# One dense tile of two RWKV quarters moved: from between the two lanes of the preparation to behind the first group of key-query products

## The chip, the cores and the metric

The kernel runs on one core of a Trainium2 chip. The metric is the device time in microseconds of one execution; of several runs the median is given. The engines are named as in the profile: PE is the matrix engine TensorE (PEld its weight loads), DVE is VectorE, ACT is ScalarE, POOL is GpSimd, and SP is the queue that issues most DMA transfers.

## The reference

One inference step of a one-layer hybrid decoder: 512 tokens of a prompt and 64 sampled tokens (8 sequences of 8), 576 in all, 1024 channels wide, in 32-bit floating point. The layer projects the normalised input once and splits the columns between two mixers. The Mamba-2 part convolves over time and runs a state space recurrence; the RWKV-7 part shifts the tokens and runs a matrix-valued recurrence per head (16 heads of 64 channels). The output projection, a SwiGLU block and a per-layer embedding follow. Cut to what the change touches:

```python
proj = hn @ w['w_in']
z, xbc, dt_raw, rw = jnp.split(proj, IN_SPLITS, axis=-1)
conv = lax.conv_general_dilated(concat([conv_buf, xbc]), conv_w, ...) + conv_b    # causal, 4 taps
xbc_act = silu(conv)                                  # 12 tiles of 128 channels
...
u = rw + (prev - rw) * shift_mu
r, k, v, w_lo, a_lo, g_lo = jnp.split(u, RWKV_SPLITS, axis=-1)
w_log = -softplus(-(w0 + tanh(w_lo) @ w2)) - 0.5      # decay, a low-rank product ("lora")
a = sigmoid(a0 + a_lo @ a2)                           # in-context rate, a second one
kk = normalised(k * k_k)
# S_t = S diag(w) - (S kk)(kk*a)^T + v k^T, read out with r; then a norm per head, a bonus, a gate
```

## The kernel before

**Tiles.** Activations lie transposed: a tile holds 128 channels by 576 tokens. A dense tile is 128 columns of the projection: 8 blocks of input channels, 2 halves of 288 tokens and 3 products each (values are split into a high and a low part, lines 228 to 230), 48 matmuls into one of the two buffers of the PSUM pool `lin`. Its weights come by DMA, are split on ACT and on DVE or POOL (line 213), and what follows depends on its kind: a tile of the convolution (`conved`) is copied out by ACT, gets three multiply-adds on DVE (line 402), a tanh and a product on ACT, two more products on DVE (lines 407 and 408) and four small copies on POOL (lines 393 to 396); a tile of the RWKV part (`shifted`) is mixed with the token before.

**Quarters and lanes.** The RWKV heads are worked in four quarters of 256 channels, `Q[0]` to `Q[3]`; the text counts them from nought as the code does, so quarters one and two are the second and the third. Each quarter has two lanes `jj` of 128 channels. Per quarter: `fill_for` runs dense tiles until the quarter's own six are there; `prep` makes decays, rates and normalised keys, lane by lane (two loras on PE, a scan at line 568, products at 572 to 588, line 591 on DVE and line 592 on POOL that write the keys `bk`); `gram` multiplies keys and queries on PE in five groups (line 620), each into a buffer of `lin`, from where DVE (line 630) and ACT with POOL (lines 641 and 645) take it out through masks; `bonus` (its products are at line 253); `solve` and `combine` invert small triangles (lines 674 to 719); `chain` runs the recurrence over chunks, each step from PE to DVE and back several times (lines 796 to 838).

**What sets the order.** The program is written in the order above, but a list scheduler puts the instructions on the engines' queues, from the written order, the pools' free buffers and a cost model. So the chain of a quarter lies beside the preparation of the next. A queue runs in its order: an instruction that waits holds what is behind it. The buffers of `lin` go round in the written order among dense tiles, loras, groups of products and the bonus.

**Where dense tiles are put.** `fill(n)` takes the next n tiles from a list that `projections` makes, whose order the change does not touch. `prep`, `gram` and `inverse` call it at eight places through `fill_at`, and the table `FP` gives for each quarter how many tiles each place takes: 0 after the sums of squares, 1 and 3 after the loras of the two lanes, 2 and 4 at the end of the two lanes, 5 and 6 after the first and the third group of products, 7 in the inverse. In quarters one and two the three tiles that the table places are all of the convolution. After the products of quarter one eight more dense tiles run, after those of quarter two six.

Of the kernel before, what the change touches and what calls it, by code (L numbers as in the profile page):

```python
# [49 lines left out]
GMA = (0, 0, 0, 0)  # L50
GMB = (0, 0, 0, 1)
FILL = (5, 5, 3, 0)
FP = ((1, 0, 1, 0, 1, 0, 0, 0), (1, 0, 1, 0, 1, 0, 0, 0), (1, 0, 1, 0, 1, 0, 0, 0), (0, 0, 0, 0, 0, 0, 0, 3))


def in_tiles(q):
# [19 lines left out]
def hybrid_step(ctx, tc, A):  # L76
# [401 lines left out]
    def fill(n=1):  # L478

        for _ in range(min(n, len(todo))):  # L480
            which, c = todo.pop(0)
            if which == "xbc":
                conved(c)
            elif which == "z":
                zed(c)
            elif which == "dt":
                dts()
            else:
                Q[which].t.append(shifted(c, which == 0, which % 2 and len(Q[which].t) > 3))

    def fill_at(s, i):
        fill(FP[s.q][i])

# [1253 lines left out]
```

## Time and profile before

| | |
|---|---|
| median of 3 runs | 1333.55 us (1332.72 to 1333.56) |
| profiled execution | 1329.48 us, span of its instructions 1327.7 us |
| mean granted clock of PE | 0.951 |
| busy in the span | PE 92%, DVE 67%, ACT 48%, POOL 46% |
| preparation and products of quarter one | about 208 to 268 us |
| preparation and products of quarter two | about 350 to 410 us |

Rows of groups give an instruction's line, engine, operation, output and inputs with their shapes, how often it ran, its busy time, the mean in ns of one, and the idle time of its engine ahead of it with what ended that. Rows of the chain of waits give the start, the time and the work that everything behind depended on. A matmul's duration reaches past the start of the next one, so the durations of a dense run add up to more than the time it takes. The clock is the share of TensorE's full clock that the chip granted.

### The profile page before, as it was taken

What the parts mean: (1) busy time and instruction counts of PE and PEld (TensorE: products, weight loads), DVE (VectorE), ACT (ScalarE), POOL (GpSimd) and SP (SyncE); (2) the same over time, 40 slices, a digit from 0 to 9 for tenths busy, and PEclk for the clock granted to TensorE, in tenths of its full rate; (3) what the DMA queues carried; (4) which work ended last, traced back from release to release, by engine and by line L of the source; (5) the groups of instructions that cost most, each with busy time, mean ns of one, the idle gap of its engine ahead of it and who ended that gap; (6) DMA issues with size and microseconds to landing.
All of it is one profiled execution on the core that took longest, in us unless ns stands there. A gap on an engine that the chain in (4) does not pass through costs nothing.

```text
span 1327.7 us, 26629 instructions
## 1 busy us (share of the span) xinstructions
PE 1224.9 (92%) x10429; PEld 1125.1 (85%) x10429; DVE 885.8 (67%) x1569; ACT 632.0 (48%) x1274; POOL 615.4 (46%) x584
## 2 busy tenths in 40 slices
PE   6897899999989978899989989999999999999997
PEld 5786797889968966788769878999999999999996
DVE  6649665878696876953456576858895138883464
ACT  6565436543654374343444364455553225553363
POOL 5426513642265136122445665647565345654642
PEclk9898999799978979979989989999999999999998
DMA  5322241334232322353454541253342224424322
GB/s 167 127 65 72 78 116 54 98 96 119 73 103 79 83 72 78 103 180 106 132 182 131 201 151 59 78 161 106 98 113 89 81 83 114 116 66 136 99 89 72
DMA packets 96764, 140.29 MB, mean 106 GB/s; under 512 B 34960, under 2 KB 39312, under 8 KB 96640
## 3 DMA queue, kind: packets, MB, share of 16 engines
q1 hardware_dynamic: 93760, 133.36, 32.6%
q0 software_dynamic: 2304, 4.72, 2.1%
q8 instruction: 82, 1.34, 0.4%
q10 hardware_dynamic: 576, 0.52, 0.1%
q14 instruction: 42, 0.34, 0.1%
HBM read 106.10 MB, written 27.75 MB: 101 GB/s over the span
## 4 chain that ended last, share of the span: by engine, by line
PE 58%; DVE 19%; ACT 6%; issue 6%; DMA 4%; POOL 3%; SPq 0%; DVEq 0%; ACTq 0%; POOLq 0%
PE lin L241 12%; PE lin L1432 11%; PE lin L228 6%; PE lin L230 6%; PE lin L229 6%; DVE h L402 2%; DVE wl L191 1%; DVE Tt L683 1%; DVE tmp L681 1%; DVE wlo L213 1%; PE lin L1577 1%; PE lin L1578 1%; PE lin L1579 1%; DVE suv L838 1%; DMA raw<-wts 1%
## 5 line engine op out<-in xcount | busy, mean ns | idle before, releaser
L213 POOL TENSOR_TENSOR wlo<-raw,whi 128x512 fp32r<-128x512 f32 (+1 forms) x92 | 125.8, 1368 | 303.6 <-ACT whi L93 235.0
L228 PE MATMUL lin<-xhi,whi 128*128 128x288 f32 (+1 forms) x784 | 242.1, 309 | 2.8 <-ACT whi L93 2.2
L230 PE MATMUL lin<-xhi,wlo 128*128 128x288 f32 (+1 forms) x784 | 240.2, 307 | 4.0 <-POOL wlo L213 2.3
L229 PE MATMUL lin<-xlo,whi 128*128 128x288 f32 (+1 forms) x784 | 239.6, 306 | 1.2 <-POOL xlo L191 1.1
L93 ACT ACTIVATE whi<-raw 128x512 fp32r<-128x512 f32 (+1 forms) x200 | 123.2, 616 | 211.0 <-PE lin L241 90.0
L228 PEld LDWEIGHTS lin<-xhi,whi 128*128 128x128 f32 (+1 forms) x784 | 149.5, 191 | 10.1 <-ACT whi L93 2.6
L230 PEld LDWEIGHTS lin<-xhi,wlo 128*128 128x128 f32 (+1 forms) x784 | 149.4, 191 | 7.9 <-POOL wlo L213 2.7
L229 PEld LDWEIGHTS lin<-xlo,whi 128*128 128x128 f32 (+1 forms) x784 | 149.4, 191 | 6.5 <-POOL xlo L191 2.4
L213 DVE TENSOR_TENSOR wlo<-raw,whi 128x512 fp32r<-128x512 f32 (+1 forms) x108 | 82.1, 761 | 74.2 <-PE lin L241 36.0
L1432 PE MATMUL lin<-T,wh 128*128 128x288 f32 x576 | 87.3, 296 | 2.0 <-DVE e L1477 1.3
L1432 PEld LDWEIGHTS lin<-T,wh 128*128 128x128 f32 x576 | 80.0, 189 | 3.2 <-DVE e L1477 1.6
L93 ACT ACTIVATE wh<-raw 128x512 fp32r<-128x512 f32 x72 | 45.1, 628 | 52.5 <-PE lin L1432 35.4
L191 POOL TENSOR_TENSOR wl<-raw,wh 128x512 fp32r<-128x512 f32 x36 | 57.3, 1592 | 11.7 <-ACT wh L93 6.2
L191 DVE TENSOR_TENSOR wl<-sw,wh 128x512 fp32r<-128x512 f32 x53 | 49.9, 941 | 9.3 <-ACT wh L93 5.2
L241 PE MATMUL lin<-ah,whi 128*128 128x288 f32 x352 | 54.7, 294 | 0.0
L241 PE MATMUL lin<-al,whi 128*128 128x288 f32 x352 | 54.4, 294 | 0.0
L241 PE MATMUL lin<-ah,wlo 128*128 128x288 f32 x352 | 54.2, 294 | 0.0
L681 DVE TENSOR_TENSOR tmp<-L,Tt 72x30 f32<-72x30 f32 (+14 forms) x120 | 49.9, 416 | 3.2
L1432 PE MATMUL lin<-T,wl 128*128 128x288 f32 x288 | 49.8, 297 | 0.6 <-DVE wl L191 0.6
L241 PEld LDWEIGHTS lin<-ah,whi 128*128 128x128 f32 x352 | 49.3, 188 | 0.0
L241 PEld LDWEIGHTS lin<-al,whi 128*128 128x128 f32 x352 | 49.2, 188 | 0.0
L241 PEld LDWEIGHTS lin<-ah,wlo 128*128 128x128 f32 x352 | 49.2, 188 | 0.0
(437 smaller groups left out, 3265.7 us busy)
## 6 DMA issues: line engine op xcount, KB each, us to landing
raw<-wts SPq DMA_DIRECT2D x271, 256.0 KB, 2.6
S<-s_wkv SPq DMA_DIRECT2D x8, 512.0 KB, 5.1
hd<-s_ssm SPq DMA_DIRECT2D x8, 512.0 KB, 4.6
o_ssm_s<-hd SPq DMA_DIRECT2D x8, 512.0 KB, 2.8
xbc_d<-E SPq DMA_DIRECT2D x12, 288.0 KB, 2.1
x<-xT SPq DMA_DIRECT2D x8, 288.0 KB
gate_d<-g SPq DMA_DIRECT2D x8, 288.0 KB, 2.5
bv_d<-rw SPq DMA_DIRECT2D x8, 288.0 KB
```

Source lines behind the costliest of these rows:

```text
L93: return S.activation(out, in_, func, bias=bias, scale=scale)
L191: eng.tensor_tensor(lo, src, hi.bitcast(F32), ALU.subtract)
L213: eng.tensor_tensor(lo[:, 0:n], raw[:, 0:n], hi[:, 0:n].bitcast(F32), ALU.subtract)
L228: T.matmul(ps[:, a:b], whi, xhi[:, a:b], start=first, stop=False)
L229: T.matmul(ps[:, a:b], whi, xlo[:, a:b], start=False, stop=False)
L230: T.matmul(ps[:, a:b], wlo, xhi[:, a:b], start=False, stop=last)
L241: T.matmul(ps[:, a:e], (hi, lo)[p][:, i * P:(i + 1) * P], xs[k + i][q][:, a:e], start=n == k + i == 0, stop=n == 2 and k + i == nk - 1, sk ...
L402: V.scalar_tensor_tensor(h[:], E[:, i:i + 600], w(i), h[:], ALU.mult, ALU.add)
L681: V.tensor_tensor(o, L[:, jx:jx + 1, jx + 1:32].to_broadcast([NB, jx, n]), Tt[:, 0:jx, jx:jx + 1].to_broadcast([NB, jx, n]), ALU.mult)
L683: V.tensor_tensor(Tt[:, 0:jx, jx + 1:32], Tt[:, 0:jx, jx + 1:32], o, ALU.subtract)
L838: V.scalar_tensor_tensor(dst, sv[h, jj, 0, e], PC[h, jj, 7 + g:8 + g], dw[h, jj], ALU.mult, ALU.add)
L1432: T.matmul(ps, (hi, lo)[p][:, k * P:(k + 1) * P], OPS[n][k][q], start=first and p == q == k == 0, stop=p == 1 and k == 3, skip_group_check ...
```

## The change

The rows of quarters one and two in the table change. The first dense tile stays after the sums of squares. The second leaves the place between the lanes (index 2) and comes at the end of the second lane (index 4); the third, which was there, comes after the first group of products (index 5). The tiles, their order among themselves and their number stay, and quarters nought and three keep their rows.

```diff
--- before.py
+++ after.py
@@ -50,7 +50,7 @@
 GMA = (0, 0, 0, 0)
 GMB = (0, 0, 0, 1)
 FILL = (5, 5, 3, 0)
-FP = ((1, 0, 1, 0, 1, 0, 0, 0), (1, 0, 1, 0, 1, 0, 0, 0), (1, 0, 1, 0, 1, 0, 0, 0), (0, 0, 0, 0, 0, 0, 0, 3))
+FP = ((1, 0, 1, 0, 1, 0, 0, 0), (1, 0, 0, 0, 1, 1, 0, 0), (1, 0, 0, 0, 1, 1, 0, 0), (0, 0, 0, 0, 0, 0, 0, 3))
 
 
 def in_tiles(q):
```

With the tile gone from between the lanes, the buffers of `lin` go round otherwise: before, the second lane's loras came after the second tile, now the four loras come one after another, then the second tile, the first group of products, the third tile and the second group.

PE, quarter one, between the lanes. `ulh` and `ull` are the operands of the loras, `xhi` and `xlo` those of a dense tile, `rx` is a transpose for the normalised keys, `um` and `suv` belong to the chain and the sampled tokens of quarter nought. Before:

```order
L530 MATMUL cb_2840<-ident,rx_2836 128x128 x4
L819 MATMUL cx_1732<-G_982,suv_1669 64x64 x4
L856 MATMUL cx_1744<-um_1745,bkt_1719 64x512
L228 MATMUL lin_2860<-xhi_350,whi_2863 128x288
L229 MATMUL lin_2860<-xlo_351,whi_2863 128x288
L856 MATMUL cx_1744<-um_1746,bkt_1719 64x512
L533 MATMUL cb_2846<-ident,rx_417_2838 128x128
L228 MATMUL lin_2942<-ulh_345,whi_2690 128x288
L229 MATMUL lin_2942<-ull_346,whi_2690 128x288
L230 MATMUL lin_2942<-ulh_345,wlo_2691 128x288
L228 MATMUL lin_2942<-ulh_345,whi_2690 128x288
L229 MATMUL lin_2942<-ull_346,whi_2690 128x288
```

With the change:

```order
L530 MATMUL cb_2840<-ident,rx_2836 128x128 x4
L228 MATMUL lin_2860<-ulh_345,whi_2690 128x288
L229 MATMUL lin_2860<-ull_346,whi_2690 128x288
L230 MATMUL lin_2860<-ulh_345,wlo_2691 128x288
L228 MATMUL lin_2860<-ulh_345,whi_2690 128x288
L229 MATMUL lin_2860<-ull_346,whi_2690 128x288
L230 MATMUL lin_2860<-ulh_345,wlo_2691 128x288
L819 MATMUL cx_1732<-G_982,suv_1669 64x64 x4
L856 MATMUL cx_1744<-um_1745,bkt_1719 64x512
L856 MATMUL cx_1744<-um_1746,bkt_1719 64x512
L533 MATMUL cb_2846<-ident,rx_417_2838 128x128
L228 MATMUL lin_2870<-ulh_345,whi_2690 128x288
```

The loras of the second lane come directly behind the transposes, and the dense tile that was begun there is gone.

PE, quarter one, around the second half of the products of group 0 (`lin_3117` before, `lin_3035` with the change). Before:

```order
L620 MATMUL lin_3117<-G_2686,bk_2986 128x128
L620 MATMUL lin_3132<-G_2686,bk_2986 128x128
L796 MATMUL cx_1859<-suv_1834,G_982 128x128
L620 MATMUL lin_3117<-G_2686,bk_2986 128x128
L620 MATMUL lin_3132<-G_2686,bk_2986 128x128
L620 MATMUL lin_3132<-G_2686,bk_2849 128x128 x2
L620 MATMUL lin_3132<-G_2686,bk_2986 128x128 x2
L804 MATMUL cx_1865<-xs_1862,TT_465 64x64 x4
L809 MATMUL cx_1870<-ar_981,suv_1834 64x64 x4
L620 MATMUL lin_3149<-G_2686,bk_2849 128x128 x2
L620 MATMUL lin_3149<-G_2686,bk_2986 128x128 x2
```

With the change:

```order
L620 MATMUL lin_3035<-G_2686,bk_2904 128x128
L804 MATMUL cx_1865<-xs_1862,TT_465 64x64
L228 MATMUL lin_3048<-xhi_461,whi_3081 128x288
L229 MATMUL lin_3048<-xlo_462,whi_3081 128x288
L230 MATMUL lin_3048<-xhi_461,wlo_3082 128x288
L228 MATMUL lin_3048<-xhi_461,whi_3081 128x288
L229 MATMUL lin_3048<-xlo_462,whi_3081 128x288
L804 MATMUL cx_1865<-xs_1862,TT_465 64x64 x3
L809 MATMUL cx_1870<-ar_981,suv_1834 64x64 x4
L620 MATMUL lin_3035<-G_2686,bk_2904 128x128
L230 MATMUL lin_3048<-xhi_461,wlo_3082 128x288
L819 MATMUL cx_1870<-G_982,suv_1834 64x64
```

The dense tile `lin_3048` runs ahead of and between the products of group 0 now; before, the products followed one another with only steps of the chain between them.

DVE, quarter two, from the second lane to the masks. `h` is the convolution's sum, `kk`, `pb`, `lo` and `bk` belong to the preparation, `suv` and `xs` to the chain, `Lst` takes the masked products. Before:

```order
L402 SCALAR_TENSOR_TENSOR h_4792<-E_4784,hw,h_4792 128x600
L586 SCALAR_TENSOR_TENSOR kk_4695<-lo_4682,kk_4695 128x576
L799 COPY xs_3520<-cx_3517 64x128
L402 SCALAR_TENSOR_TENSOR h_4792<-E_4784,hw,h_4792 128x600
L591 SCALAR_TENSOR_TENSOR bk_4709<-kk_4695,lo_4672 64x9x64 x2
L588 TENSOR_TENSOR lo_4682<-lo_4682,rw_4129 128x576
L407 SCALAR_TENSOR_TENSOR E_4784<-th_4797,h_4792 128x512
L408 SCALAR_TENSOR_TENSOR E_4784<-th_4797,h_4792 128x64
L812 TENSOR_SCALAR suv_3472<-cx_3523 64x2x64
L602 SCALAR_TENSOR_TENSOR lo_4682<-rw_4265,pv,lo_4682 128x576
L838 SCALAR_TENSOR_TENSOR suv_3538<-suv_3472,pc_2687,cx_3544 64x64 x4
L630 TENSOR_TENSOR Lst_4839<-lin_4840,dgmask 64x128 x2
```

With the change:

```order
L402 SCALAR_TENSOR_TENSOR h_4710<-E_4702,hw,h_4710 128x600
L588 TENSOR_TENSOR lo_4600<-lo_4600,rw_4129 128x576
L799 COPY xs_3566<-cx_3563 64x128
L407 SCALAR_TENSOR_TENSOR E_4702<-th_4715,h_4710 128x512
L408 SCALAR_TENSOR_TENSOR E_4702<-th_4715,h_4710 128x64
L602 SCALAR_TENSOR_TENSOR lo_4600<-rw_4265,pv,lo_4600 128x576
L213 TENSOR_TENSOR wlo_5594<-raw_5591,whi_5593 128x512
L630 TENSOR_TENSOR Lst_4757<-lin_4758,dgmask 64x128
L812 TENSOR_SCALAR suv_3538<-cx_3569 64x2x64
L402 SCALAR_TENSOR_TENSOR h_4843<-E_4835,hw,h_4843 128x600
L630 TENSOR_TENSOR Lst_4757<-lin_4758,dgmask 64x128
L402 SCALAR_TENSOR_TENSOR h_4843<-E_4835,hw,h_4843 128x600
```

Before, the last tile's convolution was over ahead of the first mask; now the tile before it stands at that place, and the last tile's stands between the masks.

## The prediction

> **What bounds the kernel now.** I read the page's totals first, then the windows of the stages that the change touches, then the chain of waits through them.
>
> ```profile
> span 1327.7 us, 26629 instructions
> ...
> PE 1224.9 (92%) x10429; PEld 1125.1 (85%) x10429; DVE 885.8 (67%) x1569; ACT 632.0 (48%) x1274; POOL 615.4 (46%) x584
> ...
> PEclk9898999799978979979989989999999999999998
> ...
> PE 58%; DVE 19%; ACT 6%; issue 6%; DMA 4%; POOL 3%; SPq 0%; DVEq 0%; ACTq 0%; POOLq 0%
> ```
>
> TensorE (PE) is the bound on average, but it holds only 58% of the chain that ends last, and its clock dips in single slices. So the average says nothing about the two places of the change, the preparations of quarters one and two. They are the first and the third row here; the second and the fourth are the stretches behind them, where dense tiles run, and the fifth is the chain of quarter two, where no dense tile is left. The last two are the groups of key-query products alone. The columns are the window, its length, each engine's busy time, the granted clock, the DMA share and GB/s.
>
> ```profile
> 208.00:268.00 60.00, 56.01 (x472) 45.94 (x471) 44.52 (x76) 38.48 (x82) 34.42 (x46) 0.83 0.24 76
> 268.00:341.00 73.00, 69.38 (x588) 64.55 (x586) 58.24 (x134) 28.13 (x68) 24.42 (x29) 1.00 0.39 113
> 350.00:410.00 60.00, 54.16 (x485) 44.31 (x483) 48.64 (x79) 38.08 (x81) 32.65 (x43) 0.83 0.23 75
> 410.00:470.00 60.00, 57.51 (x520) 52.82 (x520) 45.40 (x116) 21.52 (x56) 17.25 (x18) 0.97 0.38 104
> 470.00:527.00 57.00, 45.41 (x558) 34.02 (x554) 44.23 (x87) 34.83 (x80) 29.41 (x33) 0.88 0.19 57
> ...
> 256.00:268.00 12.00, 11.18 (x117) 9.55 (x115) 7.81 (x20) 7.19 (x21) 8.66 (x15) 0.64 0.08 27
> ...
> 399.00:410.00 11.00, 10.50 (x116) 8.95 (x112) 6.92 (x20) 7.74 (x22) 7.73 (x13) 0.75 0.06 21
> ```
>
> In both preparations the clock is 0.83, and it falls to 0.64 and 0.75 while the key-query products run: a busy TensorE there is a slow TensorE. Behind them the clock is 1.00 and 0.97 and TensorE is nearly full. The chain of waits says who holds the preparation of quarter two up (start, us, what):
>
> ```profile
> 372.63 1.54 DVE h L402
> ...
> 374.79 1.54 DVE h L402
> 376.33 2.50 DVE lo L568
> 378.83 1.86 DVE h L402
> ...
> 388.38 0.84 DVE h L402
> ...
> 391.10 0.75 DVE h L402
> ...
> 392.88 0.84 DVE h L402
> ...
> 395.19 0.76 DVE lo L588
> ...
> 396.46 1.42 DVE E L408
> ...
> 399.71 2.01 PE lin L620 x16
> ```
>
> VectorE (DVE) holds it. Six of these steps are L402, the convolution of a dense tile, which nobody in the preparation needs: it only stands on VectorE ahead of what is needed. L588 is the last VectorE work before GpSimd (POOL) makes the second half of the keys, and the products of group 0 that use it (L620) can only follow:
>
> ```profile
> 396.02 3.25 POOL L592 TENSOR_TENSOR bk<-lo,lo 64x576 f32<-64x576 f32 x2 [9.55 <-DVE lo L588]
> ```
>
> POOL had waited 9.55 us for L588 by then. Whatever convolution work leaves the queue ahead of L588 brings this point forward.
>
> **The change part by part.** Nothing is added or removed; each of the two quarters has its second dense tile moved to the end of the second lane and its third from there to behind group 0.
>
> *1. Convolutions ahead of L588.* Before, quarter two has three of them ahead of L588 but for the last L407 and L408; the order of the change has two there, with the third from the first masks (L630) on. So one tile's work leaves. Its price is in the groups of VectorE between 350 and 402 us, then between 208 and 260 us (busy, mean ns of one):
>
> ```profile
> L402 DVE SCALAR_TENSOR_TENSOR h<-E,hw,h 128x600 f32<-128x600 f32 x9 | 10.2, 1136 | 1.5 <-ACT h L93 1.4
> ...
> L407 DVE SCALAR_TENSOR_TENSOR E<-th,h 128x512 f32<-128x512 f32 x3 | 2.9, 965 | 0.0
> L213 DVE TENSOR_TENSOR wlo<-raw,whi 128x512 fp32r<-128x512 f32 x4 | 2.7, 686 | 0.7 <-ACT whi L93 0.7
> ...
> L408 DVE SCALAR_TENSOR_TENSOR E<-th,h 128x64 f32<-128x64 f32 x3 | 1.8, 616 | 0.0
> ```
>
> ```profile
> L402 DVE SCALAR_TENSOR_TENSOR h<-E,hw,h 128x600 f32<-128x600 f32 x9 | 9.4, 1040 | 1.7 <-ACT h L93 1.6
> ...
> L407 DVE SCALAR_TENSOR_TENSOR E<-th,h 128x512 f32<-128x512 f32 x3 | 3.0, 1014 | 0.0
> ...
> L408 DVE SCALAR_TENSOR_TENSOR E<-th,h 128x64 f32<-128x64 f32 x3 | 2.1, 697 | 0.0
> L213 DVE TENSOR_TENSOR wlo<-raw,whi 128x512 fp32r<-128x512 f32 x3 | 2.0, 682 | 0.0
> ```
>
> The new order takes from ahead of quarter two's L588 3 x 1.14 + 0.97 + 0.62 + 0.69 (the low part of a weight block) = 5.7 us. In quarter one the last tile's L402 stand behind L588 already; what leaves is one L402, L407, L408 and a weight split of the tile before: 1.04 + 1.01 + 0.70 + 0.68 = 3.4 us. Together -9.1 us. The other bound is 0: if something else becomes last in the lanes, all of it is lost.
>
> *2. The clock in the products.* A slow clock costs at most what is missing: 12.00 x (1 - 0.64) = 4.3 us in quarter one and 11.00 x (1 - 0.75) = 2.75 us in quarter two, 7.1 together. With a dense tile in front of the second half of group 0 TensorE is fuller there. Bounds 0 and -7.1.
>
> *3. The moved convolution beside the products.* In quarter one VectorE is busy 7.81 of 12.00 us. The tile adds about 4.9 (three L402, L407, L408 by the second set of rows), so 12.7 in 12.00; in quarter two 6.92 + 5.0 = 11.9 in 11.00. VectorE becomes the bound there and the stretch grows by 0.7 and 0.9, provided that the clock has recovered as in 2; otherwise by up to a tile's 5 us each. With the recovered clock the stage could not be shorter than that, so I take 2 and 3 together: +1.6 us. Bounds -7.1 and +10.
>
> A rule speaks against this step. Here L402 takes 1.54 to 1.86 us where POOL works beside it (the first rows of the chain) and 0.75 to 0.84 where it doesn't. The Trainium skill, "SBUF — State Buffer", section on its two sides, says that VectorE and GpSimd share one port pair under an exclusive lock, which an operation with two SBUF inputs takes against a GpSimd operation that reads SBUF, and that the loser waits for the whole instruction. By it the moved L402, beside POOL's masks, would cost 1.0 us more each, about +3 us a quarter; by the uncontended rows nothing more. The rows agree with the rule as to the doubling, but say nothing of masks as short as those; it is rival A.
>
> *4. Lanes without the tile between them.* The loras of the second lane come right behind those of the first, and wait for a buffer of the two in the lin pool, which ScalarE's tanh frees. The row of such a wait, the longest of TensorE between 208 and 269 us:
>
> ```profile
> PE lin L228 <- ACT lo L93: 1.6, 1, 1.6
> PE lin L230 <- POOL wlo L213: 1.1, 1, 1.1
> ```
>
> Behind a waiting lora stand the chain's small products of the quarter before. One more such wait of 1.6 us a quarter, of which VectorE's queue hides a part: +1 each, +2 together. Bounds 0 and, by the stretch that has no dense tiles at all, see rival B, +12.8.
>
> *5. What runs earlier.* In the new order 12 small products of the chain stand ahead of the bonus's first product (L253) in quarter one that stood behind it, and 18 in quarter two. Their groups between 268 and 341 us:
>
> ```profile
> L804 PE MATMUL cx<-xs,TT 64*64 64x64 f32 x24 | 2.3, 236 | 2.4 <-DVE xs L799 2.4
> L830 PE MATMUL cx<-suv,bkt 128*64 128x64 f32 x32 | 1.9, 234 | 0.0
> L819 PE MATMUL cx<-G,suv 128*64 128x64 f32 x32 | 2.9, 228 | 0.0
> ```
>
> At 0.23 us it is 2.8 and 4.1 us, but durations overlap: products start every 0.13 us in a dense run, so about half, 1.5 and 2.2. The stretch behind is shorter by that if TensorE ran them where it else idled. That it does is half sure: -1.9 us. Bounds 0 and -3.7.
>
> ```profile
> 205.03 0.29 PE L228 MATMUL lin<-xhi,whi 128*128 128x288 f32 x1
> 205.16 0.29 PE L229 MATMUL lin<-xlo,whi 128*128 128x288 f32 x1
> ```
>
> *Does it reach the end?* Behind the products TensorE is nearly full at clock 1.00 and 0.97, so an earlier start is an earlier end, unless the solve ends last. Its last VectorE copy is done long before its result is used (L705), 22 us in quarter two:
>
> ```profile
> L684 DVE COPY L<-Tt x1: 1091/1091/1091, 457.0 to 457.0; 36x1024 f32<-36x1024 f32 x1
> ...
> L705 PE MATMUL cx<-AA,Lst x64: 191/191/212, 479.1 to 480.1; 32*32 32x32 f32 x64
> ```
>
> In the new order its first operation (L674) stands one or two steps of the chain further back on VectorE, which this covers, as it does a shift of the whole size; the weight loads follow too, with a DMA share of 0.39 at most. The moved tile's own matmuls cost nothing extra, being moved from one TensorE-filled place to another; without that cover its 48 products are 48 x 0.13 = 6.3 us.
>
> **The sum:** -9.1 + 1.6 + 2 - 1.9 = -7.4 us. The profiled execution took 1329.48 us around its span of 1327.7, so it becomes 1322.1. The runs' median is 1333.55, 4.1 above the profiled one; the same difference gives 1326.1, and I say 1326.
>
> **Rivals.**
>
> *A, the stall only moves.* VectorE is taken out of the lanes and put between the masks, where a late L630 keeps a lin buffer and so the next group waiting. For it: 12.7 us of VectorE work in 12.00, and the doubled L402. Against: only the masks are delayed, and dense tiles are queued behind. With the extra 3 us a quarter the sum is -7.4 + 6 = -1.4; with an unrecovered clock about +1. So 1333 ± 2.7.
>
> *B, slower: the second lane loses its filler.* In the stretch from 470 us, without dense tiles, TensorE is busy 45.41 of 57.00 us at clock 0.88: 0.20 + 0.12 = 0.32 us lost in each. A lane of 12 to 20 us without a tile would lose 3.8 to 6.4 a quarter, 10.2 for both in the middle, in place of the +2 of step 4. If ScalarE's tanh or the transposes then hold the lane, half of step 1 is lost as well: -4.5 + 1.6 + 10.2 - 1.9 = +5.4, 1339. It decides once a quarter loses over 4.7 us more in the lane than step 4 has. For it: the clock is the lowest where only small products run. Against: the second tile follows at the end of the same lane, and the new order puts the loras, which are dense, there.
>
> The clock has a rule of its own: the Trainium skill, "TensorE: Matmul & The Clock Gate", section "HAM oscillation — how this bites in real kernels", asks for no TensorE idle gap over some 3.4 us. By it the waits of 1 to 2 us here would leave the clock alone, and B would lose 0.20 a us, not 0.32, so 1335; the trace differs, for the clock is 0.64 from 256 to 268 us with TensorE busy 11.18 of 12.00.
>
> *C, a larger gain.* The products run at full clock, VectorE's masks fit around the convolution and no wait is added: -9.1 - 7.1 - 3.7 = -19.9, 1314. For it: 7.1 us of missing clock. Against: VectorE's 12.7 us.
>
> *D, it does something else.* The order is made by a scheduler, and TensorE's rows differ from 218 to about 820 us. A queue that is put differently further on (the loras of quarter three) may add or take about 3 us. It widens the other cases.
>
> **How the numbers follow.** Forecast 0.54 (4 to 14 us gained, 1319.5 to 1329.5), A 0.16, B 0.20, C 0.10. A measurement of this kernel tells 0.2%, 2.7 us, from no change. Faster by more: forecast and C, 0.64; within: A, 0.16; slower: B, 0.20. The range takes in C's point and B's: 1314 to 1339, with half of each beyond, 0.15 left out; it lies inside the bounds of the steps.
>
> **What would show it.** Step 1: L588 of the second lane some 5 us nearer to the preparation's start in quarter two, some 3 us in quarter one. Steps 2 and 3: a clock near 1 from group 0 to L253, with L402 among the L630 and at about 0.8 us; at 1.5 us and more it is A. Step 4: one wait of a lora on ScalarE of under 2 us a quarter; several, with the clock under 0.8 in the second lane, are B. The end: the dense stretches as long as before, less a few us. If the time from the start of a preparation to L253 isn't shorter by 2 to 7 us in each quarter, I am wrong.

## The result, and the profile after

The change makes the kernel slower: 1346.28 us (median of 4 runs, 1342.0 to 1350.56) against 1333.13 us, a ratio of 1.0108 with a 95% interval of 1.0065 to 1.015. The profiled execution took 1344.57 us against 1329.48, with a span of 1342.8 against 1327.7. The forecast was 1326 us, in a range from 1314 to 1339.

The page of the changed kernel, the lines that answer to those shown of before:

```profile
span 1342.8 us, 26625 instructions
...
PE 1238.9 (92%) x10429; PEld 1136.9 (85%) x10429; DVE 884.5 (66%) x1569; ACT 629.9 (47%) x1272; POOL 612.3 (46%) x584
...
PEclk9897799999988976879989988999999999999998
...
PE 51%; DVE 14%; issue 4%; ACT 3%; DMA 3%; POOL 1%; SPq 0%; DVEq 0%; ACTq 0%; POOLq 0%
```

The work is the same (10429 matmuls, DVE 884.5 us against 885.8), so 15 us were added by waiting and by a slower clock. The page doesn't say where. Its last line, the chain of waits, can't be compared with that of before: its shares add up to 76%, those of before to 96%, so the chain was not followed back as far. I cut both spans at instructions that both kernels have: the first scan of a quarter (line 568), the end of line 588 in the second lane, the first product of the bonus (line 253), the first use of quarter three's solve (line 705), the end of the dense tile lin_9035, and the start of lin_9233, the first tile of the output projection's gated half that runs from its first product to its last without a stop. All in us:

| stretch | before | change | difference |
|---|---|---|---|
| start to quarter one's scan | 212.9 | 215.4 | +2.5 |
| quarter one, scan to L588 | 39.1 | 36.3 | -2.8 |
| quarter one, L588 to L253 | 16.2 | 20.1 | +3.9 |
| to quarter two's scan | 85.3 | 85.3 | 0 |
| quarter two, scan to L588 | 42.4 | 37.9 | -4.5 |
| quarter two, L588 to L253 | 14.3 | 18.3 | +4.0 |
| to quarter three's scan | 65.8 | 61.2 | -4.6 |
| quarter three, scan to L253 | 47.8 | 54.8 | +7.0 |
| to L705 | 59.2 | 60.8 | +1.6 |
| to the end of lin_9035 | 174.0 | 172.8 | -1.2 |
| to the start of lin_9233 | 47.8 | 58.7 | +10.9 |
| to the end of the span | 522.9 | 521.0 | -1.9 |

Up to quarter three's scan the change is 1.3 us ahead, although it lost 2.5 us ahead of quarter one's scan, where TensorE's order is still the same in both kernels; so much can differ between two profiles of the same order. It loses 7 us in quarter three, whose row in the table it does not touch, and 11 us some 300 us behind that, in the state space part.

The windows of these stretches, first of before and then of the change (window, length, busy times of PE, PEld, DVE, ACT and POOL, clock, DMA share, GB/s): the products of quarters one and two from L588 on, quarter three, its second half, and the stretch from the end of lin_9100 to lin_9233. lin_9100 is the last dense tile that needs nothing of the gated half; "the last dense tile" below means it.

```profile
252.10:268.20 16.10, 15.28 (x136) 12.67 (x133) 11.55 (x26) 8.80 (x25) 12.69 (x18) 0.61 0.12 37
395.90:410.20 14.30, 13.02 (x148) 11.21 (x146) 9.19 (x24) 7.91 (x23) 10.80 (x14) 0.70 0.06 23
...
476.00:523.80 47.80, 37.27 (x488) 27.91 (x488) 37.52 (x70) 27.44 (x63) 24.80 (x31) 0.86 0.16 54
500.00:524.00 24.00, 19.60 (x258) 14.05 (x258) 16.30 (x37) 10.02 (x30) 14.55 (x18) 1.00 0.21 70
770.70:804.80 34.10, 26.62 (x230) 21.84 (x228) 24.18 (x34) 25.89 (x62) 20.89 (x16) 0.85 0.43 133
```

```profile
251.80:271.90 20.10, 16.98 (x184) 13.99 (x182) 16.61 (x31) 11.54 (x32) 14.73 (x21) 1.00 0.19 58
395.20:413.50 18.30, 13.65 (x150) 10.97 (x149) 15.09 (x27) 9.69 (x27) 13.77 (x20) 0.87 0.18 61
...
474.70:529.50 54.80, 45.67 (x485) 34.45 (x483) 36.39 (x69) 26.97 (x61) 24.44 (x31) 0.69 0.14 47
504.00:524.50 20.50, 19.28 (x190) 16.82 (x190) 9.31 (x24) 6.52 (x20) 6.00 (x10) 0.51 0.16 54
778.60:821.80 43.20, 33.77 (x267) 27.08 (x266) 25.71 (x37) 26.45 (x65) 23.13 (x18) 0.76 0.42 123
```

Three things are to be seen. In the products the clock did recover, 0.61 to 1.00 and 0.70 to 0.87, and the stretches are longer all the same, with 5 and 6 us more work on DVE in them. In quarter three TensorE is busy for 8 us more with as many matmuls, because the clock was 0.51 for 20 us where it had been 1.00. (Both kernels also have half clock for 13.7 us earlier in quarter three, from 483 to 497 us; only the change falls a second time.) And behind the last dense tile the change has 37 matmuls more left to do, at a lower clock.

Two waits stand at the start of the slow stretch of quarter three, which begins in the second of them. TensorE's timeline of the change, with the idle time ahead of a row in brackets:

```profile
502.81 0.29 PE L804 MATMUL cx<-xs,TT 64*64 64x64 f32 x2 [1.37 <-DVE S L858]
...
505.22 0.58 PE L804 MATMUL cx<-xs,TT 64*64 64x64 f32 x5 [1.75 <-DVE xs L799]
```

Before, no wait between 500 and 524 us is over 1.0 us. A longer one, of 2.7 us, ends at 488 us, in the first stretch at half clock, and the clock came back 8 us behind it. For the end, the waits of TensorE from the last dense tile to lin_9233, of the change and then of before (total, times, longest):

```profile
PE d L1160 <- DMA hd<-s_ssm: 3.0, 1, 3.0
PE d L347 <- DVE rn L344: 1.9, 1, 1.9
PE y L1211 <- DVE xs L1212: 1.9, 1, 1.9
```

```profile
PE d L1204 <- ACT bc L93: 2.8, 1, 2.8
PE lin L241 <- ACT yh L93: 2.5, 2, 1.6
```

Line 1160 is the product of a sampled sequence with its loaded state, 32 matmuls each in the trace. Before, one such sequence is left behind the last dense tile; in the change two are, and the last of them waits for its state. The scheduler put them there: from 680 to 820 us its order differs, though nothing in the table concerns that part.

### The profile page after: what moved, and what is told of

It reads as the page before. It is cut to its first block, busy times and chain, and to the rows that moved or that the text cites. A ratio compares the mean times of both kernels' runs of the same rounds, so it can differ in the third digit from the quotient of the medians.

```text
span 1342.8 us, 26625 instructions
## 1 busy us (share of the span) xinstructions
PE 1238.9 (92%) x10429; PEld 1136.9 (85%) x10429; DVE 884.5 (66%) x1569; ACT 629.9 (47%) x1272; POOL 612.3 (46%) x584
## 4 chain that ended last, share of the span: by engine, by line
PE 51%; DVE 14%; issue 4%; ACT 3%; DMA 3%; POOL 1%; SPq 0%; DVEq 0%; ACTq 0%; POOLq 0%
PE lin L241 12%; PE lin L1432 10%; PE lin L230 5%; PE lin L228 4%; PE lin L229 4%; DVE wl L191 1%; PE lin L1577 1%; PE lin L1579 1%; PE lin L1578 1%; DMA raw<-wts 1%; PE cx L796 1%; DVE wlo L213 1%; PE lin L620 1%; PE cx L804 1%; DVE suv L838 1%
## 5 line engine op out<-in xcount | busy, mean ns | idle before, releaser
L213 POOL TENSOR_TENSOR wlo<-raw,whi 128x512 fp32r<-128x512 f32 (+1 forms) x92 | 124.1, 1349 | 294.5 <-ACT whi L93 254.1
L228 PE MATMUL lin<-xhi,whi 128*128 128x288 f32 (+1 forms) x784 | 246.2, 315 | 5.3 <-ACT whi L93 2.2
L230 PE MATMUL lin<-xhi,wlo 128*128 128x288 f32 (+1 forms) x784 | 243.8, 311 | 2.4 <-POOL wlo L213 2.4
L228 PEld LDWEIGHTS lin<-xhi,whi 128*128 128x128 f32 (+1 forms) x784 | 152.6, 195 | 10.7 <-ACT whi L93 2.8
L230 PEld LDWEIGHTS lin<-xhi,wlo 128*128 128x128 f32 (+1 forms) x784 | 152.4, 195 | 7.0 <-POOL wlo L213 3.5
L229 PEld LDWEIGHTS lin<-xlo,whi 128*128 128x128 f32 (+1 forms) x784 | 152.9, 195 | 4.4 <-issue 0.9
L213 DVE TENSOR_TENSOR wlo<-raw,whi 128x512 fp32r<-128x512 f32 (+1 forms) x108 | 81.0, 750 | 77.3 <-ACT whi L93 37.6
L1432 PE MATMUL lin<-T,wh 128*128 128x288 f32 x576 | 86.8, 295 | 2.0 <-DVE e L1477 1.3
L1432 PEld LDWEIGHTS lin<-T,wh 128*128 128x128 f32 x576 | 79.5, 188 | 3.2 <-DVE e L1477 1.6
L1432 PE MATMUL lin<-T,wl 128*128 128x288 f32 x288 | 49.4, 295 | 0.6 <-DVE wl L191 0.6
```

Of the source, the lines that this page charges most:

```text
L213: eng.tensor_tensor(lo[:, 0:n], raw[:, 0:n], hi[:, 0:n].bitcast(F32), ALU.subtract)
L228: T.matmul(ps[:, a:b], whi, xhi[:, a:b], start=first, stop=False)
L229: T.matmul(ps[:, a:b], whi, xlo[:, a:b], start=False, stop=False)
L230: T.matmul(ps[:, a:b], wlo, xhi[:, a:b], start=False, stop=last)
L1432: T.matmul(ps, (hi, lo)[p][:, k * P:(k + 1) * P], OPS[n][k][q], start=first and p == q == k == 0, stop=p == 1 and k == 3, skip_group_check ...
```

## The experiments

Two theories were set against each other. One: most of the loss is not made by the moved tiles but by the other order that the scheduler gives to what comes behind, in quarter three and at the end of the state space part. Two: it comes with the moved tiles, or with a clock that happened to be low.

**A barrier that makes the order behind it equal.** The edit, made to both kernels:

```diff
     while todo and todo[0][0] != "z":
         fill()
     nc.sync.dma_start(A["o_shift"], sho[:])
+    tc.strict_bb_all_engine_barrier()
     early_.close()
```

> The kernel before with one barrier of all engines at the end of the loop over quarters, ahead of the state space stage. With it that stage is scheduled afresh, and in the same order as in the next run. Theory one (the 13 us are lost far behind the change, 10 of them because the state space stage, from about 690 to 822 us, is scheduled in another order): this run is the yardstick for the next, some 10 to 25 us slower than before for the drained overlap. Theory two (the loss comes with the moved tile itself, or with a clock that happened to be low): the same yardstick.

> The change with the same barrier. From the barrier on each engine has the same instructions in the same order as in the run with the barrier alone; only quarters one to three differ. Theory one: the state space stage takes the same time in both within 1.5 us, and the whole differs from the barrier alone by the sum of the earlier stages, -3.8 us for quarters one and two and +8.5 for quarter three by the two profiles, so +3 to +6 us. Theory two: the difference stays at +13 us, 9 or more of it behind the barrier.

Measured: 1373.09 us (1.0279 of before, 1.024 to 1.0318) and 1375.11 us (1.0311, 1.027 to 1.0353). The change costs 2.0 us by the medians in place of 13, less than the two intervals can tell from nothing. The barrier itself cost close to 40 us, more than the 10 to 25 that I had expected. The stretch from the last dense tile to lin_9233, of the barrier alone and of the change with it:

```profile
815.10:850.60 35.50, 28.68 (x229) 22.77 (x229) 27.14 (x35) 26.37 (x62) 21.02 (x16) 0.82 0.43 134
```

```profile
818.00:852.90 34.90, 27.31 (x230) 21.75 (x229) 26.12 (x34) 26.11 (x62) 20.10 (x15) 0.85 0.43 134
```

With an equal order the loss at the end is gone. Quarter three, ahead of the barrier, still differs: 50.5 against 55.2 us from scan to bonus. At lin_9233 2.3 us are left of 7.1, most of the rest made up between L705 and lin_9035 (177.3 us against 180.6). That part lies behind the barrier, where both kernels have the same order, and I had expected 1.5 us of difference there at most: two profiles of the same order are 3 to 4 us apart. So the 2.0 us of the whole owe something to chance, while the end itself is alike in both. Theory two fails for the end.

**One quarter's row at a time.**

```diff
-FP = ((1, 0, 1, 0, 1, 0, 0, 0), (1, 0, 1, 0, 1, 0, 0, 0), (1, 0, 1, 0, 1, 0, 0, 0), (0, 0, 0, 0, 0, 0, 0, 3))
+FP = ((1, 0, 1, 0, 1, 0, 0, 0), (1, 0, 0, 0, 1, 1, 0, 0), (1, 0, 1, 0, 1, 0, 0, 0), (0, 0, 0, 0, 0, 0, 0, 3))
```

and, for quarter two, the new row in the third place and the old one in the second.

> The table's new row for quarter one alone. Its order in quarter three and in most of the state space stage is that of the change. Theory one: it pays in those stages as the change does, +7 in quarter three and +8 to +10 in the state space stage, less a gain of 1 to 3 us in the stages of quarters one and two: +11 to +16 us. Theory two: each row brings half, +6.5 us.

> The table's new row for quarter two alone. Quarter three has nearly the order of before (about one row in ten differs), the state space stage an order of its own. Theory one: nothing lost in quarter three (within 2 us), -1 to -3 in quarter two, and the state space stage anywhere from 0 to +10: the whole from -3 to +8 us. Theory two: +6.5 us, lost in quarter two's own stages.

Measured: quarter one alone 1348.57 us, 1.0109 (1.0073 to 1.0144), the whole loss; quarter two alone 1332.95 us, 0.9996 (0.997 to 1.0021), none. With quarter one alone, quarter three took 54.6 us from scan to bonus, and two sampled sequences were left behind the last dense tile, 42.2 us. With quarter two alone these are 50.5 and 34.8 us with one sequence left. Quarter three's clock with quarter one alone, the whole and the second half:

```profile
472.90:527.50 54.60, 45.58 (x486) 35.15 (x484) 36.14 (x69) 27.23 (x61) 24.38 (x31) 0.69 0.14 49
503.90:524.40 20.50, 20.15 (x198) 17.48 (x194) 8.74 (x24) 6.68 (x20) 6.20 (x11) 0.50 0.09 28
```

The 20 us at half clock are there again, in the same place. They are in all four profiles with the change's order in quarter three (the change, with the barrier, with quarter one's row alone, with the hold further down), and in none of the four with the order of before or nearly so (before, with the barrier, with quarter two's row alone, with the hold), where 0 to 7 us are at half clock after 497 us. The chip's chance is not what puts them there; the order is.

**The same order at the end with another change.**

```diff
-... (1, 0, 1, 0, 1, 0, 0, 0), (1, 0, 1, 0, 1, 0, 0, 0), ...
+... (1, 0, 0, 0, 2, 0, 0, 0), (1, 0, 0, 0, 2, 0, 0, 0), ...
```

> Second and third tile of quarters one and two both at the end of the second lane, none behind the first group of products. From about 680 us on each engine has the order of the change, instruction by instruction; quarter three has an order of its own. Theory one (the order of the state space stage costs 10 us): that stage takes 182 to 184 us from the first of its products (L1093) to the last product of the prompt heads (L1204), as in the change, against 172 before, and the whole is +6 to +14 us. Rival (what is lost there is lost by what runs beside it, not by the order): 172 to 175.

Measured: 1344.72 us, 1.0113 (1.0064 to 1.0163). L1093 to the last L1204 took 182.0 us. The end:

```profile
777.80:820.70 42.90, 33.65 (x267) 26.98 (x266) 26.60 (x37) 26.45 (x65) 23.10 (x18) 0.76 0.40 124
```

That is the row of the change over again, 267 matmuls and a clock of 0.76, although quarter three took only 49.4 us here. The rival, what runs beside it, falls. The products of quarters one and two, from L588 to L253, took 19.3 and 18.0 us although no tile is put behind their first group: four and three of the convolutions' L402 still ran there, behind L588.

**Only the third tile moved.**

```diff
-... (1, 0, 1, 0, 1, 0, 0, 0), (1, 0, 1, 0, 1, 0, 0, 0), ...
+... (1, 0, 1, 0, 0, 1, 0, 0), (1, 0, 1, 0, 0, 1, 0, 0), ...
```

> The second tile stays between the lanes; only the third goes from the end of the second lane to behind the first group. It does the part of the change that puts convolution work beside the products. By my prediction's sum the products' stretch grows by about 1 us a quarter and the lanes gain nothing: scan to bonus 55 to 58 us in both quarters. If the products' stretch costs the 4 us that the change shows in both quarters (L588 to L253), scan to bonus is 58 to 61. Theory one for the whole: quarter three has nearly the order of before, so within 3 us there; the state space stage has an order close to the change's except at its end, +2 to +10; total +2 to +14.

Measured: 1334.44 us, 1.0018 (0.9992 to 1.0043). Scan to bonus took 54.0 and 55.8 us, 1.3 and 0.8 less than before: scan to L588 was shorter by 2.7 us in both quarters, and the products' stretch longer by 1.4 and 1.8, where I had expected nothing of the lanes and about 1 us of the products. Quarter three took 49.1 us, and one sampled sequence was left at the end, 38.8 us. So a tile behind the first group costs less than 4 us when the tile between the lanes stays.

**A gate tile behind the first group of quarter three**, without the change and with it:

```diff
-(0, 0, 0, 0, 0, 0, 0, 3)
+(0, 0, 0, 0, 0, 1, 0, 2)
```

> The kernel before with one of the three gate tiles of quarter three moved from the inverse to behind the first group of products. The state space stage keeps nearly the order of before. Theory one: that stage 171 to 175 us; quarter three's clock was 1.00 from 500 to 524 us already, so the tile only shifts 6 us of work: scan to bonus 52 to 55 us, the stretch behind it shorter by as much, the whole within 4 us of before. Rival: quarter three gains 5 us or more.

> The change with the same tile behind the first group of quarter three. In the change the clock is 0.5 there from 504 to 524 us after two waits of 1.4 and 1.75 us. If the missing dense work is why it does not recover, the clock is near 1 behind the tile and the stretch from quarter three's scan to the solve's use (L705) is 108 to 111 us against 115.6 in the change. If the clock is set by something else, 115 to 118. The state space stage has an order of its own: 172 to 184.

Measured: 1347.07 us, 1.0137 (1.0106 to 1.0168), and 1347.65 us, 1.013 (1.01 to 1.016). Both of my expectations for quarter three were wrong. It took 62.2 and 62.9 us from scan to bonus, and with the change 120.6 from scan to L705, where 108 to 111 stood for a recovered clock and 115 to 118 for the rival. The windows in the run with the change, from the tile's second part to 4 us behind it and then the slow stretch:

```profile
496.80:507.00 10.20, 9.51 (x48) 5.02 (x46) 7.06 (x8) 4.95 (x10) 5.57 (x5) 1.00 0.19 57
510.50:530.90 20.40, 20.40 (x194) 17.43 (x190) 7.39 (x21) 6.00 (x19) 4.94 (x8) 0.50 0.12 45
```

The clock was 1.00 there and then 0.50 for as long as in the change. With the change the tile only moves the slow stretch back, by 7 to 8 us. In the kernel before it even brings one, of 17 us, that was not there without it:

```profile
522.80:539.80 17.00, 15.06 (x144) 12.76 (x142) 5.20 (x16) 5.00 (x15) 5.11 (x6) 0.50 0.18 43
```

So dense work ahead of such a stretch doesn't keep its clock up. The state space stage kept the order of before in the run without the change, and took 172.1 us from L1093 to L1204, just as before.

**Dense work held back for the end.** If the end is long because nothing dense lies beside the last heads, a tile that is held back should shorten it, in the change and in the kernel before:

```diff
-                T.matmul(ops[:, c * P:c * P + P], hin[c + 1][:, j * P:j * P + P], CT[g][:, 192 + c * P:320 + c * P],
+                marks["p", j] = T.matmul(ops[:, c * P:c * P + P], hin[c + 1][:, j * P:j * P + P], CT[g][:, 192 + c * P:320 + c * P],
...
-        linear(YR if c >= NPART else YR[6:8], ps)
+        if c == 7:
+            with tc.issue_after(marks["p", 4].ins):
+                linear(YR, ps)
+        else:
+            linear(YR if c >= NPART else YR[6:8], ps)
```

> The change with one thing more: the last dense tile ahead of the gated part of the output projection (lin_9100) may start only behind the state products of prompt head 4, so that dense work lies among the last heads. Theory one, sharpened (the change loses 8 to 9 us from the end of the last dense tile on, because two sampled sequences are left there in place of one and nothing dense lies beside them): from the end of the tile before (lin_9035) to the first tile of the gated part (lin_9233) the change takes 58.7 us and before 47.8; here 49 to 54, and the whole 5 to 9 us under the change, 1337 to 1341. Rival (the heads are bound by VectorE, ScalarE and GpSimd, and the tile only shifts): 57 to 60, the whole within 3 us of the change.

> The kernel before with the same hold. Before, one sampled sequence and the heads are left behind the last dense tile, with TensorE busy 26.6 of 34.1 us at a clock of 0.85. Theory one: 43 to 47 us from lin_9035 to lin_9233 against 47.8, the whole 1 to 5 us faster than before. Rival: 48 to 50, the whole the same or slower.

Measured: with the change 1340.96 us, 5.3 under the change, 1.0054 of before (1.0031 to 1.0077, which just overlaps the change's interval); lin_9035 to lin_9233 took 54.9 us in place of 58.7, a little above my range. Without the change 1328.58 us, 0.9954 (0.9932 to 0.9976): 40.9 us in place of 47.8, more than I had expected, and the fastest kernel of this study. Of the 6.9 us gained up to lin_9233, which is stopped once in this run, 4.8 are left at the first product of the feed-forward block (L1432). The last 27 us, up to 2 us into lin_9233:

```profile
776.00:803.00 27.00, 25.74 (x219) 22.94 (x218) 21.34 (x28) 23.61 (x54) 16.68 (x12) 0.98 0.44 131
```

TensorE is nearly full there at a clock of 0.98, where before it was busy 26.6 of 34.1 us at 0.85. The rival, that the heads are bound by the other engines, falls.

**The third tile put elsewhere.**

```diff
-... (1, 0, 1, 0, 1, 0, 0, 0), (1, 0, 1, 0, 1, 0, 0, 0), ...
+... (1, 0, 0, 0, 1, 0, 0, 1), (1, 0, 0, 0, 1, 0, 0, 1), ...
```

> The change, but the third tile of quarters one and two is put into the inverse in place of behind the first group of products. It takes the lanes' part of the change alone. If the convolution beside the products costs the 4 us a quarter that the change shows from L588 to L253, that stretch is 16 to 17 and 14 to 15 us as before, and scan to L588 36 to 40 us as in the change; scan to bonus 52 to 55 in both. If the products' stretch is longer because of the chain's products that run in it now, 19 to 21 and 18 to 19. The order at the end leaves two sampled sequences behind the last dense tile: 42 to 44 us from there to lin_9233, so the whole is +5 to +12 us by theory one.

> The third tile in the inverse and the hold together. Theory one: 5 to 9 us under the run with the third tile in the inverse alone, so about the time of before, 1329 to 1337; if the hold does nothing, the same as that run within 3 us.

Measured: 1343.14 us, 1.0062 (1.0036 to 1.0088), and with the hold 1343.96 us, 1.0091 (1.0055 to 1.0127). Without the tile behind the first group, scan to L588 took 36.4 and 34.4 us, L588 to L253 17.0 and 17.0. In quarter one that is the length of before but for 0.8, so of the change's 4 us the convolution makes 3; in quarter two it is 2.7 above before, so there it makes 1.3 and the rest has another cause, which stays open. VectorE was busy for only 10.6 of these 17.0 us in either quarter, and TensorE for 15.4 and 15.3 at a clock of 0.62 and 0.71. The tile is paid for in the inverse: 95.2 and 72.9 us to the next scan, 10 and 7 more than before. Quarter three, with an order of its own, took 44.5 us. The end has two sequences left, as expected, and took 41.8 us, just under the range. The hold shortened lin_9035 to lin_9233 from 57.4 to 50.4 us, of which 4.4 are left at L1432, and did not show in the median, where I had expected 5 to 9 us. I can't explain that; the profiled execution with the hold was 2.5 us shorter, and its runs spread from 1340.8 to 1352.56.

## Why the prediction was wrong

The sum was -7.4 us and the change measured +13. By the means below some 6 us of the gap lie in quarters one and two, 5 in quarter three and 9 at the end.

**Steps 1 and 4, the lanes: -4.4 us where they had -7.1 together.** VectorE lost the work that step 1 names: from scan to L588 it was busy for 1.7 us less in quarter one (32.02 to 30.30) and 7.4 less in quarter two (38.45 to 31.04), 9.1 in all. The lanes gained half of that. L588 came 2.8 and 4.5 us nearer to the scan in the first profile, against 3.4 and 5.7. Over all profiles with these orders the gain is smaller. Quarter one's stretch took 39.1, 39.1, 39.1, 37.6 and 37.6 us with the order of before and 36.3, 40.6, 40.6, 37.9 and 36.3 with the change's, means of 38.5 and 38.3: nothing. Quarter two's took 42.3 to 42.4 before and 37.9 to 39.0 after: -4.2. So -4.4. Not all of it is due to the tiles that left: with quarter one's row alone quarter two's stretch took 39.9 us too, with its own row as before and nearly as many convolutions ahead of L588; why stays open. In quarter one another wait took the place of the VectorE work that left, which is the other bound of step 1; see rival B below.

**Steps 2 and 3, the products: set at a fifth of what they measured.** The clock recovered as said in the first profile and bought nothing, because in the change TensorE is not what ends last there: with the barrier quarter two's products had a clock of 0.64 and took 19.0 us, hardly more than the 18.3 at 0.87. VectorE's waits in quarter one's products from L588 on, of before and of the change:

```profile
DVE Lst L630 <- PE lin L620: 1.8, 3, 1.2
DVE Lst L630 <- ACT G L93: 1.6, 2, 1.1
DVE suv L838 <- PE cx L830: 0.4, 1, 0.4
```

```profile
DVE E L407 <- ACT th L93: 0.9, 1, 0.9
DVE Lst L630 <- ACT G L93: 0.8, 1, 0.8
DVE Lst L630 <- PE lin L620: 0.7, 1, 0.7
```

I had set VectorE's work, 12.7 us, against a stretch of 12.00 and added the excess alone, as if all its idle time could be filled. But most of its waits remain when work is added: in quarter one it had 5.1 us more to do (11.55 to 16.61), its idle time fell only from 4.6 to 3.5, and the stretch grew by 4.0. Steps 2 and 3 together were +1.6 for both quarters; they measured +4.0 and +4.1, in the five and four profiles with these orders (20.1 to 20.3 against 16.2, 18.3 to 19.0 against 14.3 and 14.4). Of quarter two's only 1.3 us went away with the tile in the inverse. This is rival A's mechanism, VectorE's work between the masks, at somewhat more than its price (3 us a quarter on top of the +1.6), but not by the longer L402 from which A had that price; see the two rules.

**Step 5: right in its direction, at more than its size.** From quarter two's L253 to quarter three's scan the change's order was 3 to 5 us shorter, more than the -1.9. With it, the sum for quarters one and two is about -1 us where I had -7.4.

**Rival B: the wait came, in another place.** Not a lora waits for ScalarE, but the transposes of the second lane's keys (L530) for VectorE's L525. Between 230 and 246 us, in the change and then with quarter one's row alone:

```profile
PE cb L530 <- DVE rx L525: 2.1, 1, 2.1
```

```profile
PE cb L530 <- DVE rx L525: 3.5, 1, 3.5
```

Before, the longest wait from 208 to 269 us was 1.6. In the second of these runs the clock fell to half behind the wait:

```profile
237.70:244.50 6.80, 6.02 (x26) 6.00 (x27) 3.94 (x9) 2.36 (x6) 1.60 (x5) 0.50 0.14 42
```

and scan to L588 took 40.6 us. With the barrier and the change it went the same way: a wait of 3.5 us, half clock for 6.8, 40.6 us. So quarter one had some of what rival B said, 2 to 4 us of it; the loss of the whole did not hang on it. B's own threshold is off by step 4's term: -7.4 is used up when each quarter loses 3.7 us more than step 4 has, 4.7 in all, and not 4.7 more.

**What failed most is rival D.** It gave an order that is put differently further on "about 3 us" and let it widen the other cases. It was worth 5 us in quarter three by the means (7 in the first two profiles) and 9 at the end, and both times the first reason was there to be read: quarter three has no dense tile for its products, and its clock in the chain's stretch was 0.88; the end has its last dense tile 34 us ahead of where dense work starts again. Rows of TensorE differing "from 218 to about 820 us" were named, but the place where a small difference becomes a large one, where the dense work runs out, was not looked for. The runs settle the end: equal order, equal time (35.5 and 34.9 us); the order of the change under another table, 42.9; one sequence left, 34.1 to 38.8 us in seven profiles, two left, 41.8 to 43.2 in four. For quarter three they show that the order decides (47.8 to 51.9 us in four profiles with that of before or nearly so, 54.6 to 55.2 in four with the change's) by way of the clock. What in the order makes the clock fall stays open: that the two waits at the start of the slow stretch are its cause was not tested, since no run took them away alone.

**The two rules.** The moved L402 took 0.82 to 1.14 us beside POOL's masks, so the price of 1 us more each, by the Trainium skill's "SBUF — State Buffer", section on its two sides, and the exclusive lock there, was not paid there. Part of it was paid by another: VectorE's L408, 0.22 us where POOL is idle, ended within 0.1 us of POOL's operation. The kernel before has two such in the two quarters, of 1.43 us at 234.00 and 1.42 at 396.46, the change four, of 1.42 to 1.80. A row of before with POOL idle, and quarter one's rows of VectorE and of POOL in the change:

```profile
248.28 0.22 DVE L408 SCALAR_TENSOR_TENSOR E<-th,h 128x64 f32<-128x64 f32 x1
```

```profile
254.30 1.46 DVE L408 SCALAR_TENSOR_TENSOR E<-th,h 128x64 f32<-128x64 f32 x1
...
266.34 1.80 DVE L408 SCALAR_TENSOR_TENSOR E<-th,h 128x64 f32<-128x64 f32 x1
```

```profile
251.85 3.83 POOL L592 TENSOR_TENSOR bk<-lo,lo 64x576 f32<-64x576 f32 x2 [6.07 <-DVE lo L588]
...
266.91 1.15 POOL L641 TENSOR_TENSOR G<-G,gmask 128x512 f32<-128x512 f32 x1
```

There the rule and the trace agree. Not each meeting costs it, though: at 302.94 us in the change L408 took 0.21 us while POOL's L213 is shown from 302.68 for 1.63 us. The Trainium skill's rule on idle gaps over some 3.4 us ("TensorE: Matmul & The Clock Gate", section "HAM oscillation — how this bites in real kernels") does not cover what was seen: the clock fell to 0.51 at waits of 1.37 and 1.75 us, with small products between them, and stayed there for 20 us with TensorE busy 19.28 of 20.50.

## What to carry to other kernels

Where a scheduler sets the order, a change of one place is a change of every place behind it: compare the orders of the two kernels at the points where the dense work runs out, and count what is left there, before costing the edit itself. A barrier put into both kernels behind the edit makes the order behind it equal, and so tells an edit's own effect from what the scheduler made of it, as far as two profiles of one order agree (here to 3 or 4 us). Work added to an engine that waits in step with others does not fill its idle time: here 5.1 and 5.9 us more of VectorE's work made the stretches 4.0 us longer each, although VectorE had been idle for 4.6 and 5.1 us in them.

## What the runs showed of the hardware that was not expected

A stretch of small products stayed at half clock for 20.4 or 20.5 us, with TensorE busy 94% or more of it, in quarter three of five kernels, and a dense tile that ended 7 us ahead of it at a clock of 1.00 did not prevent it. The kernel before has as long a stretch at half clock in quarter two, from 384 to 404.5 us, with TensorE busy for 17.7 us of it. The same order in the lanes of quarter one took from 36.3 to 40.6 us in five profiles, so a single profile can't tell a gain of 3 us there. And a VectorE operation of 0.22 us can take 1.8 us where GpSimd is in the middle of others.
